# An in-projection that reads x in ready-made columns, takes four latent tiles in flight, and leaves the rope tables to the next stage

## The chip, the core and the metric

The kernel runs on one core of a Trainium2 chip. The time of a kernel is the device time of one launch in microseconds (us); times that are compared are medians over several executions. A core has a matmul engine (PE in the profile, with its weight loads as PEld), a vector engine (DVE, `V` in the code), an activation engine (ACT, `A`), a third elementwise engine (POOL, `G`) and a queue that issues most transfers (SP, `nc.sync`). Each engine works its own instructions off in the order in which the program wrote them, and waits for others by semaphores.

## The reference

One layer of a streaming encoder on x of 1024 rows by 1024 columns, all in float32:

```
h    = rmsnorm(x, g_mix);  proj = h @ w_in              # 1024 x 1952
c_q, c_kv, k_rope, qkv = proj[:, :256], [256:384], [384:416], [416:1952]
q    = rmsnorm(c_q) @ w_uq;  kv = rmsnorm(c_kv) @ w_ukv # 8 heads; per-head rmsnorm, rope
A    = block-causal attention(q, kv);  B = 9-chunk band attention(qkv) with a learned bias
x   += concat(rmsnorm(A), rmsnorm(B)) @ w_out
x   += w_down(silu(g) * u),  [g|u] = causal conv3(rmsnorm(x) @ w_up)
```

## The kernel before

Every float32 product is made of three faster ones (`mm3`, L136): each operand is split into a high part (rounded to the fast format) and a low part (what is left), and PE adds high by high, high by low and low by high. A split is one ACT or DVE instruction that writes the high part and one that subtracts it from the source.

The order on every engine is the order in which the Python code issues instructions (`manual_schedule`). Tiles come from pools: 28 buffers of 128x1024 (`blk`), 10 of 128x512 (`p2`), and banks of the matmul engine's accumulator. The stages that matter here:

**In-projection to the latents (loop at L408).** x comes in 8 tiles of 128 rows. PE needs x with its columns on the partitions, so `trans_x` (L213) transposes the eight 128x128 pieces of a tile on PE into a bank; ACT writes the high part and DVE the low part (`hTh`, `hTl`). `split_wlat` (L160) scales the four weight pieces of 416 columns by `g_mix` on ACT in place and splits them on DVE. `latent(t)` (L231) makes 24 matmuls of 416 columns, then ACT evicts the result, scales it by the row's 1/rms (`rsx`, from `norm_x`) and squares it in three pieces with an accumulator each; POOL turns each sum into 1/rms by a multiply-add and a power (`rsq`, L189), and DVE scales the latent. `trans_c(t)` (L252) transposes the latent on PE in three pieces, and ACT and DVE split it. In iteration t the order is `latent(t)`, `trans_x(t+2)`, `norm_x(t+2)`, `trans_c(t-1)`, and in iterations 2 to 5 one part of the rope tables: cosines and sines of the positions, with a transpose of small tables (L313 to L315), ten small DVE operations on the angles and a sine on ACT. `rope_k` (eight POOL operations) stands behind the loop.

**Up-projection of the latents (`up_mla`, L440, eight tiles)**, then **the other 1536 columns of the in-projection (L804)** in 32 steps, one for each 128 rows of 512 weight columns. In step i `load_wc(i+2)` loads weights that `split_wc(i+1)` (L533) splits: ACT scales in place, DVE casts the high part, DVE subtracts, in steps 26 to 31 POOL (`WC_LO_G`, L53). Steps from 3 on carry pieces of `side`, first of all `post_mla` (L489), which applies the rope tables on POOL.

**Entry to the attention (from step 22).** Between the matmuls of the last steps `prep` (L639) sets up the first two heads: transposes, splits into a tile `set`, and two copies on chip, `dup_q` (L678) and `dup_k` (L684), issued by POOL. The first products of the score maxima (`mx`, L724) read what `dup_k` writes.

The rest (attention, out-projection, a feed-forward part that is most of the time) is not touched.

Of the kernel before, what the change touches and what calls it, by code (L numbers as in the profile page):

```python
# [10 lines left out]
F32 = mybir.dt.float32  # L11
# [41 lines left out]
WC_LO_G = range(26, 32)  # L53
# [25 lines left out]
def trunk(ctx, tc, a, out):  # L79
# [62 lines left out]
    xt = {}  # L142
# [62 lines left out]
    gmix, rsx = scol(8), scol(8)  # L205
# [24 lines left out]

    def latent(t):  # L231
        p = bank()
        o = p[:, :LW]
        for k in range(8):
            h, c = hTv(0, t // 4), hTv(1, t // 4)
            s0 = (t % 4) * 128
            mm3(o, h[:, k, s0:s0 + 128], c[:, k, s0:s0 + 128], wlh[k // 2][:, k % 2, :LW], wll[k // 2][:, k % 2, :LW],
                k == 0, k == 7)
        l = blk(F32, "lat")
        lat[t] = l  # L240
        A.activation(l[:, :LW], o, AF.Copy, scale=rsx[:, t:t + 1])
        c = scol(4)
        A.activation(l[:, 512:768], l[:, 0:256], AF.Square, accum_out=c[:, 0:1])
        A.activation(l[:, 512:640], l[:, 256:384], AF.Square, accum_out=c[:, 1:2])
        A.activation(l[:, 512:544], l[:, 384:416], AF.Square, accum_out=ss_kr[:, t:t + 1])
        rsq(c[:, 2:3], c[:, 0:1], 1.0 / 256)
        rsq(c[:, 3:4], c[:, 1:2], 1.0 / 128)
        V.scalar_tensor_tensor(l[:, 0:256], l[:, 0:256], c[:, 2:3], lora_g[:, 0:256], op0=ALU.mult, op1=ALU.mult)
        V.scalar_tensor_tensor(l[:, 256:384], l[:, 256:384], c[:, 3:4], lora_g[:, 256:384], op0=ALU.mult, op1=ALU.mult)
        V.tensor_copy(KR[:, t, :], l[:, 384:416])  # L250

    def trans_c(t):  # L252
        p = bank()
        l = lat[t]
        for k in range(3):
            T.transpose(p[:, k * 128:(k + 1) * 128], l[:, k * 128:(k + 1) * 128], ident)
        if t < 6:
# [24 lines left out]
    def load_rows():  # L282
        rows = rope["rows"] = blk(F32, "rows")
        G.memset(rows[:, 0:256], 0.0)
        nc.sync.dma_start(rows[0:8, 256:384].bitcast(I32), a["positions"].rearrange("a (t p) -> (a t) p", p=128))
        nc.sync.dma_start(rows[:, 512:544], dap(a["g_mla_q"], NOPE, [[0, 128], [1, 32]]))
        nc.sync.dma_start(rows[:, 544:576], dap(a["g_mla_k"], NOPE, [[0, 128], [1, 32]]))
        nc.sync.dma_start(rows[0:128, 0:128], dap(a["conv_w"], 0, [[128, 128], [1, 128]]))
        nc.sync.dma_start(rows[0:4, 128:256], dap(a["conv_w"], 128 * 128, [[128, 4], [1, 128]]))
        nc.sync.dma_start(rows[4:48, 128:256], dap(a["conv_b"], 0, [[128, 44], [1, 128]]))  # L290
        nc.sync.dma_start(rows[48:52, 128:256], dap(a["g_out_mla"], 0, [[128, 4], [1, 128]]))
        nc.sync.dma_start(rows[52:56, 128:256], dap(a["g_out_ca"], 0, [[128, 4], [1, 128]]))
        nc.sync.dma_start(rows[56:57, 128:224], a["g_mla_q"])
        nc.sync.dma_start(rows[57:58, 128:224], a["g_mla_k"])
        nc.sync.dma_start(rows[58:59, 128:192], a["g_ca_q"])
        nc.sync.dma_start(rows[59:60, 128:192], a["g_ca_k"])
# [13 lines left out]
    def rope_angles():  # L310
        rows = rope["rows"]
        p = ps()
        T.transpose(p[:, 0:128], rows[:, 0:128], ident)  # L313
        T.transpose(p[:, 128:192], rows[0:64, 128:256], ident[0:64, 0:64])
        T.transpose(p[:, 192:200], rows[0:8, 384:512], ident[0:8, 0:8])  # L315
        V.tensor_copy(cols, p[:, 0:192])
# [5 lines left out]
        V.tensor_copy(pos, p[:, 192:200])  # L322
# [58 lines left out]
    def split_wq(i):  # L381
# [9 lines left out]
        V.tensor_tensor(l, s, f(h), op=ALU.subtract)  # L391
# [5 lines left out]
    T.transpose(p[:, 0:8], grow, ident[0:8, 0:8])  # L397
# [1290 lines left out]
```

## Time and profile before

| | |
|---|---|
| median of 3 runs | 1278.47 us (1276.62 to 1279.32) |
| profiled execution, own time | 1279.72 us |
| its span on the core | 1278.0 us, so 1.7 us lie around it |
| PE busy in the span | 1226.7 us (96%) |
| DVE, ACT, POOL busy | 942.8, 653.0, 699.1 us |
| granted clock of PE, mean over the span | 0.993 of full speed |

Times in the profile count from the start of the span. PE's matmuls overlap, so an instruction's own duration is longer than the distance to the next; what a matmul costs in a stream is that distance. [...]

### The profile page before, as it was taken

To read this page: it belongs to the slowest core of one execution; us is meant where nothing else is said; L and a number is where in the kernel's file an instruction comes from. 1 tells how busy PE (TensorE), PEld (TensorE's weight loads), DVE (VectorE), ACT (ScalarE), POOL (GpSimd) and SP (SyncE) were. 2 spreads that over 40 slices of the span, in tenths; PEclk is the share of its full clock that TensorE was granted. 3 is DMA by queue.
4 is the path that set the end of the run, shared out by engine and by line. 5 is a ranking of instruction groups with operands and counts; after the bars stand their busy time and mean duration, and the time that the engine had idled before them with its cause. 6 is when DMAs were issued, how large, how long until landed. Compare 5 with 4: busy or idle time off the path is not lost.

```text
span 1278.0 us, 17884 instructions
## 1 busy us (share of the span) xinstructions
PE 1226.7 (96%) x5920; PEld 1010.0 (79%) x5920; DVE 942.8 (74%) x1630; ACT 653.0 (51%) x1377; POOL 699.1 (55%) x715
## 2 busy tenths in 40 slices
PE   7999998899998998999989999999999999999998
PEld 7888886778786876788768888888888888878887
DVE  4786865778888895465898776677677677788983
ACT  6681443687877787504554444344344344434442
POOL 3578733455565668303568776676676650425630
PEclk9999998999999999999999999999999999999999
DMA  5101123111111121273513423323323246933253
GB/s 199 56 27 50 58 63 78 26 43 22 35 43 43 39 68 51 80 251 132 182 49 116 129 69 99 123 91 116 115 68 106 92 154 246 381 92 111 63 194 128
DMA packets 101316, 130.58 MB, mean 102 GB/s; under 512 B 11783, under 2 KB 60519, under 8 KB 101223
## 3 DMA queue, kind: packets, MB, share of 16 engines
q1 hardware_dynamic: 99431, 125.17, 30.3%
q0 software_dynamic: 1792, 4.26, 1.7%
q8 instruction: 47, 0.77, 0.3%
q14 instruction: 46, 0.38, 0.1%
HBM read 93.27 MB, written 31.81 MB: 98 GB/s over the span
## 4 chain that ended last, share of the span: by engine, by line
PE 50%; DVE 6%; POOL 2%; issue 2%; ACT 1%; POOLq 0%; DVEq 0%; ACTq 0%
PE pb L137 11%; PE pb L138 11%; PE pb L139 11%; PE ps L137 6%; PE ps L139 5%; PE ps L138 5%; DVE as L1404 1%; DVE ps L1420 1%; DVE x2b L1420 0%; DVE h L1188 0%; DVE as L1403 0%; DVE as L1405 0%; DVE as L1406 0%; POOL plo L932 0%; DVE wring L1595 0%
## 5 line engine op out<-in xcount | busy, mean ns | idle before, releaser
L932 POOL TENSOR_TENSOR plo<-misc,phi 128x512 fp32r<-128x512 f32 (+3 forms) x116 | 119.3, 1031 | 58.1 <-ACT phi L917 41.5
L1365 ACT ACTIVATE u<-ps,cols 128x1024 f32<-128x1024 f32 x44 | 53.2, 1208 | 177.7 <-DVE ps L1420 177.7
L137 PE MATMUL ps<-hq,wop 128*128 128x512 f32 x344 | 135.0, 392 | 2.6 <-ACT wop L1336 1.5
L139 PE MATMUL ps<-hq,wop 128*128 128x512 f32 x344 | 134.1, 390 | 1.2 <-DVE wop L1341 1.2
L138 PE MATMUL ps<-hq,wop 128*128 128x512 f32 x344 | 134.0, 390 | 0.1
L138 PE MATMUL pb<-wring,aring 128*128 128x512 f32 x308 | 120.1, 390 | 3.0 <-DVE wring L1595 3.0
L137 PE MATMUL pb<-wring,aring 128*128 128x512 f32 x308 | 120.0, 390 | 0.3 <-DVE x2b L1420 0.3
L139 PE MATMUL pb<-wring,aring 128*128 128x512 f32 x308 | 119.8, 389 | 0.0
L1341 POOL TENSOR_TENSOR wop<-S,wop 128x512 fp32r<-128x512 f32 x42 | 63.4, 1509 | 96.4 <-ACT wop L1336 96.4
L137 PE MATMUL pb<-hq,wop 128*128 128x512 f32 x264 | 103.5, 392 | 2.3 <-ACT wop L1336 2.3
L139 PE MATMUL pb<-hq,wop 128*128 128x512 f32 x264 | 103.7, 393 | 0.2 <-DVE wop L1341 0.2
L138 PE MATMUL pb<-hq,wop 128*128 128x512 f32 x264 | 103.2, 391 | 0.0
L1592 DVE TENSOR_TENSOR aring<-ast,aring 128x512 fp32r<-128x512 f32 x77 | 70.0, 909 | 36.8 <-ACT aring L1591 36.7
L1591 ACT ACTIVATE aring<-ast 128x512 fp32r<-128x512 f32 x77 | 48.5, 630 | 94.7 <-PE pb L138 75.4
L914 ACT ACTIVATE misc<-pb 128x512 f32<-128x512 f32 (+3 forms) x116 | 56.3, 485 | 48.4 <-PE pb L900 20.0
L137 PEld LDWEIGHTS ps<-hq,wop 128*128 128x128 f32 x344 | 64.6, 188 | 19.8 <-DVE ps L1420 4.9
L139 PEld LDWEIGHTS ps<-hq,wop 128*128 128x128 f32 x344 | 64.6, 188 | 15.2 <-DVE wop L1341 1.5
L137 PE MATMUL pb<-wh,hTh 128*128 128x512 f32 x192 | 76.3, 397 | 0.0
L138 PE MATMUL pb<-wl,hTh 128*128 128x512 f32 x192 | 76.0, 396 | 0.1
L139 PE MATMUL pb<-wh,hTl 128*128 128x512 f32 x192 | 75.5, 393 | 0.0
L138 PEld LDWEIGHTS ps<-hq,wop 128*128 128x128 f32 x344 | 64.6, 188 | 13.8 <-DVE hq L1224 0.6
L192 POOL TENSOR_TENSOR stat<-stat,mhalf 128x1 f32<-128x1 f32 (+2 forms) x50 | 71.6, 1431 | 4.2
(349 smaller groups left out, 3649.6 us busy)
## 6 DMA issues: line engine op xcount, KB each, us to landing
wstage<-in_w_up_dram SPq DMA_DIRECT2D x43, 512.0 KB
ast<-act_scratch SPq DMA_DIRECT2D x77, 256.0 KB
act_scratch<-as SPq DMA_DIRECT2D x44, 256.0 KB
wd<-in_w_down_dram SPq DMA_DIRECT2D x44, 256.0 KB
act_scratch<-u SPq DMA_DIRECT2D x33, 256.0 KB
x<-in_x_dram SPq DMA_DIRECT2D x16, 512.0 KB
ws<-in_w_in_dram SPq DMA_DIRECT2D x32, 256.0 KB
x_scratch<-x SPq DMA_DIRECT2D x14, 512.0 KB
```

Source lines behind the costliest of these rows:

```text
L137: T.matmul(o, lh, rh, start=start, stop=False)
L138: T.matmul(o, lh, rl, start=False, stop=False)
L139: T.matmul(o, ll, rh, start=False, stop=stop)
L192: G.tensor_tensor(dst, dst, mhalf[:, :n], op=ALU.pow)
L914: A.activation(p32[:, w], o[:, w], AF.Exp, scale=sc_)
L932: e.tensor_tensor(plo[:, w], p32[:, w], f(phi[:, w]), op=ALU.subtract)
L1341: (V if n in W_LO_V or (j, n) in W0_LO_V else G).tensor_tensor(lo, s, f(hi), op=ALU.subtract)
L1365: A.activation(u, U, AF.Identity, scale=convw(2, c), bias=convb(c))
L1404: V.tensor_tensor(s[1], s[0], A11, op=ALU.subtract)
L1420: V.tensor_tensor(d, x_, y, op=op)
L1591: A.activation(ah, s, AF.Copy)
L1592: V.tensor_tensor(al, s, f(ah), op=ALU.subtract)
```

## The change

The host now lays x out a second time, in columns (`x_cols`), and `g_mix`, the positions and the small tables as columns too. Each x tile is loaded twice: `xT` (columns) for `split_x`, which takes the place of `trans_x` and needs no PE, and `x` (rows) for `norm_x`. The loads stand in the order in which they are needed. Eighteen matmuls of the identity by itself run ahead of the first latent (`WARM`). The latent's work is cut into `latent`, `norm_lat`, `scale_lat`, `trans_c` and `split_c`, which in iteration t work on tiles t, t-1, t-1, t-2 and t-3. One square of 416 columns and three sums on DVE replace three squares with accumulators. The rope tables move to steps 0 to 3 of the next stage, and `split_wlat` and `split_wc` take two instructions in place of three (ACT writes the scaled high part, DVE makes scaled source minus high part); `WC_LO_G` is gone. The low part of `split_wq` moves from DVE to POOL.

```diff
-WC_LO_G = range(26, 32)
+WARM = 18
...
+    def load_xT(t, n=1):
+        xT[t] = blk(F32, "xT")
+        w = 1024 // n
+        for i in range(n):
+            nc.sync.dma_start(xT[t][:, i * w:i * w + w], a["x_cols"][t][:, i * w:i * w + w])
...
-        for k in range(2):
-            A.activation(s[:, k], s[:, k], AF.Copy, scale=gmix[:, 2 * i + k:2 * i + k + 1])
-        V.tensor_copy(wlh[i][:, :, :LW], s)
-        V.tensor_tensor(wll[i][:, :, :LW], s, f(wlh[i][:, :, :LW]), op=ALU.subtract)
+        for k in ks:
+            g = gmix[:, 2 * i + k:2 * i + k + 1]
+            hi = wlh[i][:, k, :LW]
+            A.activation(hi, s[:, k], AF.Copy, scale=g)
+            V.scalar_tensor_tensor(wll[i][:, k, :LW], s[:, k], g, f(hi), op0=ALU.mult, op1=ALU.subtract)
+
+    gmix = const([128, 8], F32, "gmix")
+    nc.sync.dma_start(gmix, a["g_mix_cols"])
     load_wlat(0)
-    load_wlat(1)
+    load_xT(0)
+    for i in range(1, 4):
+        load_wlat(i)
+    load_xT(1)
+    load_x(0)
+    load_xT(2)
     load_x(1)
...
-    def trans_x(src, t):
-        p = ps()
-        p3 = p.rearrange("p (k s) -> p k s", k=8)
-        for k in range(8):
-            T.transpose(p[:, k * 128:(k + 1) * 128], src[:, k * 128:(k + 1) * 128], ident)
+    def split_x(t, k0=0, k1=8):
+        p3 = xT[t].rearrange("p (k s) -> p k s", k=8)[:, k0:k1]
...
+    def norm_lat(t):
+        l = lat[t] = blk(F32, "lat")
+        c = clat[t] = scol(4)
+        A.activation(l[:, :LW], plat.pop(t)[:, :LW], AF.Copy, scale=rsx[:, t:t + 1])
+        sq = l[:, 512:512 + LW]
+        A.activation(sq, l[:, :LW], AF.Square)
+        for d_, c0, c1 in ((c[:, 0:1], 0, 256), (c[:, 1:2], 256, 384), (ss_kr[:, t:t + 1], 384, 416)):
+            V.reduce_sum(d_, sq[:, c0:c1], axis=AX)
         rsq(c[:, 2:3], c[:, 0:1], 1.0 / 256)
         rsq(c[:, 3:4], c[:, 1:2], 1.0 / 128)
...
         V.tensor_copy(h, s)
-        V.tensor_tensor(l, s, f(h), op=ALU.subtract)
+        G.tensor_tensor(l, s, f(h), op=ALU.subtract)
...
+    for _ in range(WARM):
+        T.matmul(p[:, 0:128], ident, ident, start=True, stop=True)
+    split_wlat(0)
+    split_x(0)
+    for i in range(1, 4):
         split_wlat(i)
+    split_x(1)
     norm_x(0)
...
+        latent(t)
+        if t >= 2:
+            trans_c(t - 2)
+        if t >= 1:
+            norm_lat(t - 1)
+        if t >= 3:
+            split_c(t - 3)
+        if t + 2 < 8:
+            split_x(t + 2)
+        if t + 1 < 8:
+            norm_x(t + 1)
         if t >= 4 and t < 7:
             split_wq(t - 4)
...
+            scale_lat(t - 1)
+    trans_c(6)
+    norm_lat(7)
+    split_c(5)
+    split_c(6)
+    scale_lat(7)
...
-            k = steps[i][1]
-            A.activation(s, s, AF.Copy, scale=gmix[:, k:k + 1])
+            g = gmix[:, steps[i][1]:steps[i][1] + 1]
             wh, wlo = p2(F32R, "wh"), p2(F32R, "wl")
-            V.tensor_copy(wh, s)
-            (G if i in WC_LO_G else V).tensor_tensor(wlo, s, f(wh), op=ALU.subtract)
+            A.activation(wh, s, AF.Copy, scale=g)
+            V.scalar_tensor_tensor(wlo, s, g, f(wh), op0=ALU.mult, op1=ALU.subtract)
...
+        if i < 4:
+            rope_tables(i)
+        if i == 3:
+            rope_k()
         if i:
             split_wc(i + 1)
```

What this does to the order on the engines shows at three places.

PE, between the third and the fourth latent before (`x` is the tile of rows that is transposed, `pb` an accumulator bank):

```order
L137 MATMUL pb_288<-wlh_130,hTh_89 128x416
L138 MATMUL pb_288<-wll_131,hTh_89 128x416
L139 MATMUL pb_288<-wlh_130,hTl_90 128x416
L217 MATMUL ps_325<-identr,x_211 128x128 x8
L256 MATMUL pb_340<-identr,lat_252 128x128 x3
L137 MATMUL pb_374<-wlh_112,hTh_89 128x416
```

PE at the same place after:

```order
L137 MATMUL pb_243<-wlh_142,hTh_94 128x416
L138 MATMUL pb_243<-wll_143,hTh_94 128x416
L139 MATMUL pb_243<-wlh_142,hTl_95 128x416
L273 MATMUL pb_268<-identr,lat_220 128x128 x3
L137 MATMUL pb_301<-wlh_122,hTh_94 128x416
```

The eight transposes of x are gone from PE, and the latent that is transposed is one tile older than before.

POOL at the entry to the attention before (`set` is the first head's tile, its two DMAs are `dup_q` and `dup_k`, `wl` the low part of a step's weights):

```order
L594 MEMSET set_2093 32x1024
L681 MEMSET set_2093 32x1024
L678 DMA set_2093<-set_2093 64x1024
L540 TENSOR_TENSOR wl_2119<-ws_2082,wh_2118 128x512
L684 DMA set_2093<-set_2093 64x1024
L540 TENSOR_TENSOR wl_2145<-ws_2115,wh_2144 128x512
```

POOL there after:

```order
L607 MEMSET set_2021 32x1024
L694 MEMSET set_2021 32x1024
L691 DMA set_2021<-set_2021 64x1024
L697 DMA set_2021<-set_2021 64x1024
L760 DMA set_2021<-mrow 1x8x128
```

The second copy no longer stands behind a subtraction of weights; the six subtractions are on DVE.

DVE in steps 2 and 3 of the next stage after (`rope` holds the angles, `wl_1180` is read by PE in step 3, `wl_1223` in step 4):

```order
L342 SCALAR_TENSOR_TENSOR rope_1069<-rope_1069 128x256 x5
L343 TENSOR_SCALAR rope_1069<-rope_1069 128x128
L344 TENSOR_SCALAR rope_1069<-rope_1069 128x256
L553 SCALAR_TENSOR_TENSOR wl_1180<-ws_1123,gmix,wh_1179 128x512
L354 TENSOR_TENSOR ropetabs_100<-rope_1069,rows_417 128x128
L355 TENSOR_TENSOR ropetabs_100<-rope_1069,rows_417 128x128
L356 TENSOR_TENSOR ropetabs_100<-rope_1069,rows_417 128x128
L357 TENSOR_TENSOR ropetabs_100<-rope_1069,rows_417 128x128
L553 SCALAR_TENSOR_TENSOR wl_1223<-ws_1164,gmix,wh_1222 128x512
```

The reduction of the angles now stands ahead of the weights of step 3, and the tables ahead of those of step 4; before, these were in the in-projection loop.

## Rows read from the trace of the kernel before

**Rows 1.** Busy time by stretch; columns: length, PE, PEld, DVE, ACT, POOL, clock, DMA share, GB/s.

```profile
22.60:58.00 35.40, 34.88 (x209) 33.48 (x208) 23.53 (x57) 24.68 (x65) 18.02 (x52) 1.00 0.28 101
58.00:88.00 30.00, 28.79 (x150) 26.27 (x149) 24.64 (x86) 24.50 (x108) 21.86 (x29) 1.00 0.04 10
88.00:206.60 118.60, 118.52 (x527) 96.74 (x525) 82.28 (x143) 45.85 (x102) 78.06 (x87) 1.00 0.22 61
...
210.80:216.30 5.50, 5.50 (x15) 4.41 (x16) 2.40 (x9) 0.00 (x0) 1.28 (x1) 0.50 0.15 38
```

**Rows 2.** Timeline of PE in the in-projection: start, duration, instruction, [idle before].

```profile
8.96 1.94 PE L217 MATMUL ps<-identr,x 128*128 128x128 f32 x8 [2.09 <-DMA x<-in_x_dram]
...
14.17 0.55 PE L138 MATMUL pb<-wll,hTh 128*128 128x416 f32 x1
...
14.52 0.55 PE L139 MATMUL pb<-wlh,hTl 128*128 128x416 f32 x1
...
22.43 0.36 PE L139 MATMUL pb<-wlh,hTl 128*128 128x416 f32 x1
...
23.74 0.43 PE L137 MATMUL pb<-wlh,hTh 128*128 128x416 f32 x1
...
28.35 1.03 PE L217 MATMUL ps<-identr,x 128*128 128x128 f32 x8
...
29.22 0.49 PE L256 MATMUL pb<-identr,lat 128*128 128x128 f32 x3
...
35.27 0.27 PE L313 MATMUL ps<-identr,rows 128*128 128x128 f32 x1
...
35.83 0.46 PE L137 MATMUL pb<-wlh,hTh 128*128 128x416 f32 x1
```

**Rows 3.** Waits of PE up to 300 us: total, times, longest.

```profile
PE pb L724 <- DMA set<-set: 4.2, 1, 4.2
...
PE pb L137 <- DVE cTl L264: 1.2, 1, 1.2
```

**Rows 4.** Same columns as the first group, for the first loads (last column GB/s).

```profile
0.00:3.00 3.00, 0.00 (x0) 0.00 (x0) 0.23 (x1) 1.28 (x1) 0.74 (x7) 1.00 0.30 63
3.00:9.00 6.00, 2.18 (x10) 1.82 (x11) 1.20 (x2) 2.09 (x4) 0.00 (x0) 1.00 1.02 377
```

**Rows 5.** Groups of instructions in the first 62 us: busy us, mean ns.

```profile
L192 POOL TENSOR_TENSOR stat<-stat,mhalf 128x1 f32<-128x1 f32 x24 | 15.9, 664 | 2.0
...
L221 ACT ACTIVATE hTh<-ps 128x1024 fp32r<-128x1024 f32 x8 | 8.1, 1009 | 4.8 <-PE ps L217 4.8
...
L222 DVE TENSOR_TENSOR hTl<-ps,hTh 128x1024 fp32r<-128x1024 f32 x8 | 9.8, 1219 | 2.8 <-ACT hTh L221 2.8
...
L248 DVE SCALAR_TENSOR_TENSOR lat<-lat,stat,lorag 128x256 f32<-128x256 f32 x8 | 3.9, 483 | 13.1 <-POOL stat L192 13.1
...
L249 DVE SCALAR_TENSOR_TENSOR lat<-lat,stat,lorag 128x128 f32<-128x128 f32 x8 | 2.8, 352 | 4.8 <-POOL stat L192 4.8
```

**Rows 6.** Timeline of ACT and of POOL at the entry to the attention.

```profile
202.66 0.59 ACT L669 ACTIVATE set<-pb 64x512 fp32r<-64x512 f32 x1
...
203.81 1.28 POOL L540 TENSOR_TENSOR wl<-ws,wh 128x512 fp32r<-128x512 f32 x1 [1.04 <-DVE wh L539]
...
205.05 0.58 POOL L684 DMA_DIRECT2D set<-set  x1
```

**Rows 7.** All eight `dup_k` copies of the kernel (line L684).

```profile
DMA to landing us min/median/max: 2.9/3.0/5.6
```

**Rows 8.** Timeline of DVE: first and last of the angles' reduction, eleven instructions.

```profile
45.94 0.22 DVE L331 TENSOR_SCALAR rope<-rope 128x128 f32<-128x128 f32 x1
...
49.82 0.29 DVE L341 TENSOR_SCALAR rope<-rope 128x256 f32<-128x256 f32 x1
```

**Rows 9.** Timeline of POOL: the seventh rope job of `side`.

```profile
135.14 3.45 POOL L501 TENSOR_TENSOR rt<-nqk,ropetabs 128x128 f32<-128x128 f32 x4 [5.09 <-DVE nqk L493]
```

**Rows 10.** Timeline of POOL: one power in the in-projection's sixth iteration.

```profile
53.80 1.93 POOL L192 TENSOR_TENSOR stat<-stat,mhalf 128x1 f32<-128x1 f32 x1
```

More of the change, by code (lines that the diff above doesn't have):

```diff
@@ L229, in trunk @@
     ss_kr = scol(8)
+    plat, clat = {}, {}
     def latent(t):
-        p = bank()
-        o = p[:, :LW]
+        p = plat[t] = bank()
         for k in range(8):
@@ L236, in latent, with scale_lat @@
             s0 = (t % 4) * 128
[L237 to L245, printed above, removed]
+            mm3(p[:, :LW], h[:, k, s0:s0 + 128], c[:, k, s0:s0 + 128], wlh[k // 2][:, k % 2, :LW],
+                wll[k // 2][:, k % 2, :LW], k == 0, k == 7)
+    def norm_lat(t):
[6 more added lines that the diff above has]
+            V.reduce_sum(d_, sq[:, c0:c1], axis=AX)
         rsq(c[:, 2:3], c[:, 0:1], 1.0 / 256)
         rsq(c[:, 3:4], c[:, 1:2], 1.0 / 128)
+    def scale_lat(t):
+        l, c = lat[t], clat[t]
         V.scalar_tensor_tensor(l[:, 0:256], l[:, 0:256], c[:, 2:3], lora_g[:, 0:256], op0=ALU.mult, op1=ALU.mult)
@@ L250, in latent @@
         V.tensor_copy(KR[:, t, :], l[:, 384:416])
+    pcT = {}
     def trans_c(t):
-        p = bank()
+        p = pcT[t] = bank()
         l = lat[t]
@@ L256, in trans_c, with split_c @@
             T.transpose(p[:, k * 128:(k + 1) * 128], l[:, k * 128:(k + 1) * 128], ident)
+    def split_c(t):
+        p = pcT.pop(t)
         if t < 6:
@@ L283, in load_rows @@
         rows = rope["rows"] = blk(F32, "rows")
[L284 to L285 removed]
+        nc.sync.dma_start(cols[:, 0:188], a["cols"])
+        nc.sync.dma_start(rows[:, 0:8].bitcast(I32), a["pos_cols"])
         nc.sync.dma_start(rows[:, 512:544], dap(a["g_mla_q"], NOPE, [[0, 128], [1, 32]]))
         nc.sync.dma_start(rows[:, 544:576], dap(a["g_mla_k"], NOPE, [[0, 128], [1, 32]]))
[L288 to L296, printed above, removed]
     def rope_tables(part):
@@ L310, in rope_angles @@
     def rope_angles():
[L311 to L316, printed above, removed]
         V.tensor_tensor(gsc[0:64, 0:1], cols[0:64, GQ:GQ + 1], cols[0:64, GK:GK + 1], op=ALU.mult)
@@ L321, in rope_angles @@
         pos = rt[:, 512:520]
-        V.tensor_copy(pos, p[:, 192:200])
+        V.tensor_copy(pos, rope["rows"][:, 0:8].bitcast(I32))
         inv = rt[:, 528:544]
@@ L396, in trunk @@
     p = ps()
-    T.transpose(p[:, 0:8], grow, ident[0:8, 0:8])
-    V.tensor_copy(gmix, p[:, 0:8])
-    trans_x(xt[0], 0)
-    for i in range(4):
+    for _ in range(WARM):
[3 more added lines that the diff above has]
+    for i in range(1, 4):
         split_wlat(i)
+    split_x(1)
     norm_x(0)
@@ L404, in trunk @@
     nc.sync.dma_start(lora_g[:, 256:384], dap(a["g_kv_lora"], 0, [[0, 128], [1, 128]]))
-    trans_x(xt[1], 1)
-    norm_x(1)
     for t in range(8):
         if t + 3 < 8:
-            load_x(t + 3)
-        if t == 1:
-            load_rows()
+            load_xT(t + 3)
+        if t + 2 < 8:
+            load_x(t + 2)
         if t == 3:
             load_wq()
+        if t == 5:
+            load_rows()
+        latent(t)
[5 more added lines that the diff above has]
+            split_c(t - 3)
+        if t + 2 < 8:
+            split_x(t + 2)
+        if t + 1 < 8:
+            norm_x(t + 1)
         if t >= 4 and t < 7:
             split_wq(t - 4)
-        latent(t)
-        if t + 2 < 8:
-            trans_x(xt[t + 2], t + 2)
-            norm_x(t + 2)
         if t >= 1:
-            trans_c(t - 1)
-        if 2 <= t < 6:
-            rope_tables(t - 2)
-    rope_k()
+            scale_lat(t - 1)
[4 more added lines that the diff above has]
+    scale_lat(7)
     side = []
@@ L775, in trunk @@
             trans_c(7)
+            split_c(7)
         if t == 2:
@@ L1678 @@
     arrays, args = {}, {}
+    inputs = {n: np.asarray(v) for n, v in inputs.items()}
+    pad = [np.pad(inputs[n].reshape(1, -1), ((0, 0), (0, 128 - inputs[n].size)))
+           for n in ("g_mla_q", "g_mla_k", "g_ca_q", "g_ca_k")]
+    inputs["cols"] = np.concatenate([inputs[n].reshape(-1, 128) for n in ("conv_w", "conv_b", "g_out_mla", "g_out_ca")]
+                                    + pad).T
+    inputs["pos_cols"] = inputs["positions"].reshape(NT, 128).T
+    inputs["x_cols"] = inputs["x"][0].reshape(NT, 128, 8, 128).transpose(0, 3, 2, 1).reshape(NT, 128, D)
+    inputs["g_mix_cols"] = inputs["g_mix"].reshape(8, 128).T
     for n, v in inputs.items():
```

34 lines of the change are left out of this document (15 added, 19 removed).

## The prediction

> **What bounds the kernel now.** First I read the table of engines by stretch [rows 1]. PE is busy for 34.88 of the 35.40 us of the later in-projection, for 28.79 of 30.00 in the up-projection and for 118.52 of 118.60 in the 32 steps that follow; no other engine comes near. From 22.6 us to the entry of the attention the time is therefore PE's own: an instruction taken from PE is time gained, and work taken from DVE, ACT or POOL is worth only what PE waited for it. Three places are different.
>
> The first 22.6 us, read from the timeline of PE [rows 2]: PE waits 2.09 us for the second tile of x, then works latent(0) with matmuls .35 us apart (14.17 to 14.52), and latent(1)'s last one starts at 22.43. In a stream later on 24 matmuls take 28.35 - 23.74 = 4.61 us, .19 apart. So the start is set by loads, by splits and by a slow clock together.
>
> The second is up_mla(0), where PE waits 1.2 us for the last split of a latent [rows 3].
>
> [...]
>
> **The change, part by part.** All sums are against the profiled execution's own 1279.72 us; the runs' median is 1.25 lower.
>
> *Start.* By the traffic [rows 4], 3.0 x 63 GB/s = .19 MB came up to 3.0 us and then .377 MB each us. Before, x(0) with g_mix (.528 MB) is through at 3.9 and x(1), at 1.904 MB, at 7.55; PE sees x(1) at 8.96, so 1.4 us later [rows 2]. After, xT(0) ends at .954 MB (5.0), the last weights at 2.23 MB (8.4), xT(1) at 2.756 MB (9.8). With .8 to 1.4 us until it is seen, xT(0) is there at 5.9 to 6.4 and xT(1) at 10.6 to 11.2. ACT's high part takes 1.01 and DVE's low part 1.22 [rows 5]: latent(0) can start at 7.2 and has its low part at 8.4. Behind that DVE has six of the eight new weight instructions of 416 columns. Their form's rows are .483 for 256 columns and .352 for 128 [rows 5], so .131 for 128 more, and .65 for 416 is my estimate: 6 x .65 = 3.9, to 12.3. The low part of xT(1) is done at 13.5. Only each third matmul of latent(1) needs that, so it starts some .4 earlier and ends near 13.1 + 4.5 = 17.6, where before it ended at 22.6. **-5.0.** [...]
>
> The 18 WARM matmuls run ahead of that, on a tile that waits for no load. No row has a plain float32 matmul of 128 columns. A transpose of 128 is .11 (.87 for eight, from 28.35 to 29.22 [rows 2]), which gives 2 us below; .25 for each, as if it took two to three passes, gives 4.5. Begun within the first 2 us, they end between 4 and 6.5, before latent(0) can start. Even at .5 each they would end near 11, and latent(1) would lose under 1.5, since DVE holds it to 13.1.
>
> *Transposes.* Eight for a tile cost .87 [rows 2]. Those of tiles 0 and 1 lie in the start. Of the other six, that of x(2) stood ahead of 22.6 and is counted there; five in the stretch 22.6 to 58 are removed: 5 x .87 = 4.35. The rope transposes take 35.83 - 35.27 = .56. **-4.9**, between 0 and -4.9 as far as other engines keep up. They have the room: DVE is busy 23.53 and ACT 24.68 of 35.40 [rows 1]; of that the rope tables leave. What the new order adds is one latent of distance to norm_lat, trans_c and split_c, 4.5 us for each, so that a chain of POOL's powers has longer. PE's idle .52 in this stretch goes too: **-.5**.
>
> *Up-projection.* The wait of 1.2 was for the last latents. After, seven of the eight latents are transposed before up_mla(0), and norm_lat(7) and scale_lat(7) stand ahead: **-.9** (-.5 to -1.2). But trans_c(6) now stands directly behind latent(7), and waits until POOL has made the powers of latent 6, which had one latent's time; a chain of evict, square, three sums, two times two POOL instructions of .66 [rows 5] and two scales is some 5.5 us against 4.5 of cover: **+.5** (0 to +1.5).
>
> *Rope tables in steps 0 to 3.* They take 4.2 us of DVE (45.94 to 50.11 [rows 8]) ahead of wl(3) in step 2, and four products ahead of wl(4). A step is 118.60/32 = 3.7 us of PE on the average, and DVE works 82.28 of 118.60 there [rows 1] and loses 32 x some .3 by splitting with one instruction instead of two. The splits run a step ahead of PE. I work out that wl(3) is finished some 3 us ahead of its use: **0** (0 to +3). The rope jobs on POOL come later, by up to 5.4 us; the seventh waited 5.09 for DVE anyway [rows 9]: 0. The split itself (one instruction less) frees DVE and ACT, which PE does not wait for: 0; the cover is PE's 118.52 of 118.60.
>
> *Entry.* Before, ACT writes the high part at 202.66 to 203.25; POOL then has wl from 203.81 to 205.09, and issues `dup_k` at 205.05 [rows 6]. A copy takes 2.9 to 5.6 us from issue to landing [rows 7]; this one was the long one, since PE went on at 210.8. After, `dup_k` stands right behind `dup_q` and is issued near 203.3: 1.75 earlier. With a landing of 3 us it would be there at 206.3, before PE is through with the steps (206.6); I take the wait to go from 4.2 to 1.0, since something of the longer landing was the traffic around it, and it need not go: **-3.2** (0 to -4.2). A shorter wait should spare part of the dip; half of the 2.7 is my choice: **-1.5** (0 to -2.7). That PE stays at full clock through a gap is shown once, in the wait of 1.2 us in up_mla(0): the stretch 58 to 88 has 1.00 throughout [rows 1, 3].
>
> Sum: -5.0 - 4.9 - .5 - .9 + .5 - 3.2 - 1.5 = -15.5, so 1264.2 on the profile's scale and **1263.0** on that of the median.
>
> **The rivals.**
>
> *The entry stays as it is.* dup_k's landing is governed by the traffic then and not by its issue, or another part of `set` is late. For it: 5.6 is far from the median of 3.0 [rows 7], and the stream of loads runs on. Against it: an issue 1.75 earlier is plain in POOL's order. Price 3.2 + 1.5 = 4.7: 1267.7.
>
> *POOL holds the in-projection.* It gets three subtractions of `split_wq`, at 1.28 for 512 columns [rows 6], in iterations 4 to 6. A power took 1.93 there once [rows 10], against .66 in the mean [rows 5]: while DVE worked on two operands from the core's memory. After, all x splits of DVE read such operands, where before one came from an accumulator bank. Each latent has three powers; all stretched to 1.93 make its chain 3.8 longer, with a subtraction ahead of it 5.1. Of the two latents of time that trans_c has, 9.2 us, the chain of some 5.5 leaves 3.7: only the three iterations with subtractions would wait, 1.4 us each and as much again in what they pass on to up_mla(0): +5, 1268. Against it: not all powers meet such a split. [...]
>
> *Rope holds the steps.* wl(3) comes behind 4.2 us of angles, and if my margin of 3 us is wrong PE waits in step 3: +3, 1266.
>
> [...]
>
> **How the numbers follow.** The forecast has 55%, with its own range of 1261 to 1266. The entry unchanged has 20% (1267.7), POOL 13% (1268), rope 7% (1266), the clock 4% (1294), and 1% is left for a change that is eaten without trace. The lower end, 1259.5, takes the whole wait (-1.0 more), the whole dip (-1.2) and the better start and up-projection (-.5 and -.8); the upper, 1269.0, holds the entry or POOL with a little more. About 0.2% (2.6 us) is what a measurement of this kernel can tell from no change. Faster by over that: .95; within it .01; slower .04.
>
> **What the profile would show.** Start: latent(1)'s last matmul at about 17.6, spacing .19 from the first or after a few matmuls. Transposes: up_mla(0) starts near 58 - 10.4 + .5 = 48, and no idle row in the loop. Entry: the wait on `mx` for `dup_k` at 1 us or gone, and the row with clock .50 shorter, near 195. Rope: no wait of PE on wl in steps 2 to 5. Wrong is the forecast if PE waits for lat or cT in the loop (POOL), if `mx` still waits 4 us, or if a stretch ahead of 40 us has a clock of .50.

## The result, and the profile after

The changed kernel takes 1270.16 us (median of 4 runs, 1268.70 to 1271.62) against 1278.89 for the kernel before beside it: a ratio of .9934 [.9921, .9947], 8.7 us less. In a second set of five runs it took 1270.95. The forecast was 1263.0, which is 15.9 us below that median (its sum was 15.5). So the gain is real and about half of what the sum gave, and the time lies above the stated range.

The profiled execution has a span of 1269.9 us, 8.1 below the one before. Its timeline of PE shows where (start, duration, instruction, idle before and what ended it):

```profile
8.46 0.43 PE L137 MATMUL pb<-wlh,hTh 128*128 128x416 f32 x1
...
14.27 0.45 PE L139 MATMUL pb<-wlh,hTl 128*128 128x416 f32 x1 [0.62 <-DVE hTl L231]
...
18.32 0.35 PE L139 MATMUL pb<-wlh,hTl 128*128 128x416 f32 x1
...
49.19 0.41 PE L273 MATMUL pb<-identr,lat 128*128 128x128 f32 x2 [1.40 <-ACT cT L283]
...
50.16 0.33 PE L273 MATMUL pb<-identr,lat 128*128 128x128 f32 x1 [0.57 <-DVE lat L264]
...
50.25 0.42 PE L137 MATMUL pb<-wq,cT 128*128 128x384 f32 x1
...
184.63 0.50 PE L138 MATMUL pb<-wl,hTh 128*128 128x512 f32 x1 [1.21 <-DVE wl L553]
...
189.31 0.50 PE L138 MATMUL pb<-wl,hTh 128*128 128x512 f32 x1 [0.74 <-DVE wl L553]
...
202.97 0.76 PE L737 MATMUL pb<-set 128*128 128x256 f32 x2 [3.61 <-DMA set<-set]
```

The first matmul of latent(0) starts at 8.46, the last one of latent(1) at 18.32; at 50.25 begins up_mla(0). Against [rows 1, 2] and the wait of [rows 3] this gives the ledger of the profile, stage by stage:

| stage, on PE | before | after | moved | forecast |
|---|---|---|---|---|
| start, to the last matmul of latent(1) | 22.43 | 18.32 | -4.1 | -5.0 |
| from there to up_mla(0) | 35.57 | 31.93 | -3.6 | -4.9 (-4.9 - .5 + .5) |
| up_mla, to the first step | 30.00 | 28.59 | -1.4 | -.9 |
| steps, to the end ahead of `mx` | 118.6 | 120.52 | +1.9 | 0 |
| wait of `mx` for `dup_k` | 4.2 | 3.61 | -.6 | -3.2 |
| clock behind it and the rest | 1067.2 | 1066.93 | -.3 | -1.5 |

The row of the steps ends ahead of the first product of `mx`; the last 22 of the steps' 192 groups of three matmuls stand behind it, in the last row.

The same by stretches (length, PE, PEld, DVE, ACT, POOL, clock, DMA share, GB/s):

```profile
18.70:47.30 28.60, 28.60 (x160) 28.16 (x160) 20.40 (x49) 19.58 (x34) 25.24 (x38) 1.00 0.59 226
50.25:78.84 28.59, 28.59 (x148) 26.29 (x149) 24.89 (x88) 23.07 (x102) 18.40 (x21) 1.00 0.07 20
78.84:199.36 120.52, 118.55 (x527) 96.92 (x525) 82.72 (x139) 47.23 (x102) 88.70 (x110) 1.00 0.21 57
199.36:202.97 3.61, 0.01 (x1) 0.04 (x1) 0.00 (x0) 0.00 (x0) 0.00 (x0) 0.86 0.94 198
202.97:208.40 5.43, 5.43 (x14) 4.38 (x15) 2.73 (x9) 0.72 (x1) 0.00 (x0) 0.50 0.15 42
```

These rows answer to [rows 1]. POOL is busy for 25.24 of 28.60 us in the in-projection, where it had been 18.02 of 35.40. In the steps PE is idle for 2 us of 120.52, where it had missed .1. The stretch behind the entry has the clock at .50 for 5.4 us, as before.

### The profile page after: what moved, and what is told of

The parts are those of the page before. It is cut to its first block, busy times and chain, and to the rows that moved or that the text cites. A ratio compares the mean times of both kernels' runs of the same rounds, so it can differ in the third digit from the quotient of the medians.

```text
span 1269.9 us, 17774 instructions
## 1 busy us (share of the span) xinstructions
PE 1221.0 (96%) x5888; PEld 1004.7 (79%) x5888; DVE 940.8 (74%) x1623; ACT 648.8 (51%) x1338; POOL 704.6 (55%) x710
## 4 chain that ended last, share of the span: by engine, by line
PE 50%; DVE 8%; issue 2%; ACT 1%; POOL 1%; DVEq 0%; POOLq 0%; ACTq 0%
PE pb L139 11%; PE pb L138 11%; PE pb L137 11%; PE ps L137 6%; PE ps L139 5%; PE ps L138 5%; DVE ps L1438 1%; DVE as L1422 1%; DVE hq L1242 1%; POOL plo L950 1%; DVE wop L1359 1%; DVE h L1206 0%; DVE as L1421 0%; DVE as L1423 0%; DVE as L1424 0%
```

## The experiments

All are the changed kernel with one edit, unless said otherwise. Single executions differ by several us in parts that no edit touches: what stands behind the first product of `mx` took 1064.8 to 1068.1 us in seven profiled executions whose edit, if any, lies ahead of it, and the way from the last matmul of latent(7) to up_mla(0) took 2.97 to 4.87 us in eight that have the changed kernel's code there. Medians of a few runs, taken in different sets, therefore blur what is worth 2 us; each verdict rests on the place in the trace first and on the time second.

**Three places were open:** 2 us ahead of up_mla(0), 1.9 us in the steps, and the entry.

**1. One subtraction given back to DVE.** POOL's rows around the wait at 49.19 in the changed kernel:

```profile
45.23 2.38 POOL L394 TENSOR_TENSOR wkl<-wks,wkh 128x1024 fp32r<-128x1024 f32 x1
47.70 0.19 POOL L203 TENSOR_SCALAR stat<-stat 128x1 f32<-128x1 f32 x1
47.97 0.55 POOL L204 TENSOR_TENSOR stat<-stat,mhalf 128x1 f32<-128x1 f32 x1
...
49.17 0.55 POOL L204 TENSOR_TENSOR stat<-stat,mhalf 128x1 f32<-128x1 f32 x1
```

The subtraction of `split_wq`'s third piece lies in front of the two powers of latent 6, at 47.97 and 49.17. The edit:

```diff
-        G.tensor_tensor(l, s, f(h), op=ALU.subtract)
+        (V if i == 2 else G).tensor_tensor(l, s, f(h), op=ALU.subtract)
```

> The changed kernel, with the low part of the third piece of split_wq (1024 columns, iteration 6) on DVE again instead of POOL; all else as changed. Theory: in the changed kernel POOL is busy with that subtraction for 2.38 us (45.23 to 47.61) just when the powers of latent 6 are due, DVE waits 2.8 us for them, and PE waits 1.40 and .57 us in trans_c(6). Then both waits of PE shrink to under .4 together, up_mla(0) starts near 48.4 instead of 50.25, and the time is 1.9 us below the changed kernel's, near 1268.3. Rival: the chain of latent 6 (evict, square, sums, two powers, two scales) is too long for one latent of cover whatever POOL does first: the waits keep at least 1.2 us and the time stays within .8 us of the changed kernel's 1270.2.

Measured: 1269.17 (.9935 [.9913, .9958]); PE still waits 1.35 and .57. up_mla(0) starts at 49.52, but only because latent(7) ended .7 us earlier in this execution: from latent(7)'s last matmul it is 3.10 us, as against 3.15. The theory in this form fell: the subtraction held DVE for 1.23 us ahead of its scales, one power of POOL beside it took 1.53 us, and POOL was at work up to the powers of latent 6 all the same. What was left was a backlog.

**2. One power less for each latent**, and **3. all of `split_wq` on DVE again**:

```diff
-        rsq(c[:, 2:3], c[:, 0:1], 1.0 / 256)
-        rsq(c[:, 3:4], c[:, 1:2], 1.0 / 128)
+        G.tensor_scalar(c[:, 2:3], c[:, 0:1], 1.0 / 256, EPS, op0=ALU.mult, op1=ALU.add)
+        G.tensor_scalar(c[:, 3:4], c[:, 1:2], 1.0 / 128, EPS, op0=ALU.mult, op1=ALU.add)
+        G.tensor_tensor(c[:, 2:4], c[:, 2:4], mhalf[:, 0:2], op=ALU.pow)
```

```diff
-        G.tensor_tensor(l, s, f(h), op=ALU.subtract)
+        V.tensor_tensor(l, s, f(h), op=ALU.subtract)
```

> The changed kernel, with the two powers of a latent made by one instruction of two columns on POOL instead of two of one column; all else as changed. The run with one subtraction given back to DVE kept PE's waits ahead of trans_c(6), so the theory now is a backlog: POOL works without a gap from about 30 to 50 us, and the powers of latent 6 stand at its end, whatever piece is taken out near it. A power less for each latent (about .63 us with the gap behind it, seven times) shortens the backlog by some 4 us: PE's waits ahead of trans_c(6) (1.97 us in the changed kernel, 3.4 in two of the runs since) fall below .8, from the last matmul of latent(7) to up_mla(0) it takes 1.5 us or less instead of 3.15, and the time is 1.5 to 2.5 below 1270.2. Rival: the latency of one latent's own chain sets it; the waits stay at 1.5 or more and the time within .8 of 1270.2.

> The changed kernel, with the low parts of all three pieces of split_wq on DVE again, as before the change. Theory of the backlog on POOL: 6 us of POOL's work between 35 and 48 us go, POOL has idle time in iterations 5 to 7, and from the last matmul of latent(7) to up_mla(0) it takes 1.6 us or less, where it took 3.15 in the changed kernel and 1.16 with the powers merged. Rival: the subtractions of two operands on DVE (about 1 us each) hold POOL as much as they free it, as in the run with one of them: 2.7 or more.

All waits of PE between latent(6) and the steps, first with merged powers, then with `split_wq` on DVE:

```profile
47.33 0.52 PE L274 MATMUL pb<-identr,lat 128*128 128x128 f32 x3 [0.22 <-DVE lat L264]
...
49.33 0.50 PE L137 MATMUL pb<-wkh,cT 128*128 128x512 f32 x1 [0.42 <-DVE cT L285]
```

```profile
49.31 0.50 PE L137 MATMUL pb<-wkh,cT 128*128 128x512 f32 x1 [0.83 <-DVE cT L284]
```

From the last matmul of latent(7) to up_mla(0) it takes 1.16 and .77 us, where it took 3.15 (2.97 to 4.87 in the eight executions with the changed kernel's code there). A wait of .4 or .8 comes up in up_mla(0) instead, for the split of a latent; to the first step it is 30.39 and 30.38 us, against 31.55 to 35.69 in the eight. So both rivals fall, and that of run 1 with them. The times are 1269.46 (.9942 [.9928, .9957]), which is less of a gain than forecast and within the .8 us that the rival had named, and 1267.74 (.9928 [.9914, .9941]). With merged powers the first product of `mx` comes 2.0 us sooner (200.96), but what stands behind it took 1.2 us longer.

The place is settled by the trace. Here is the last power of latent 6 on POOL in runs 1, 2 and 3:

```profile
48.45 0.55 POOL L204 TENSOR_TENSOR stat<-stat,mhalf 128x1 f32<-128x1 f32 x1
```

```profile
45.96 0.70 POOL L260 TENSOR_TENSOR stat<-stat,mhalf 128x2 f32<-128x2 f32 x1
```

```profile
45.56 0.55 POOL L204 TENSOR_TENSOR stat<-stat,mhalf 128x1 f32<-128x1 f32 x1
```

Counted from the start of latent(7)'s last matmul (46.42, 46.44 and 46.41) it ends 2.58 us behind it, .22 behind it, and .30 ahead of it; in the eight it is 2.44 to 4.30 behind. From latent(1)'s last matmul to the end of that power POOL is busy for 26.5 to 28.0 us in the eight, and for 27.8, 20.7 and 23.6 in the three runs. So one subtraction of 2.4 us given away took nothing off POOL that shows, since its other instructions became longer beside DVE's (the one power 1.53 in place of .55); of all three, 6.1 us, some 3 to 4.5 came off, since a power beside two of DVE's took up to 2.13. POOL had more work than the shorter stage leaves it.

**4. The normalisation one job later, and 5. three instructions for a split again.** In the steps, the rows of DVE and of POOL ahead of PE's wait at 184.63:

```profile
178.01 1.23 DVE L541 TENSOR_TENSOR ca<-ca,stat 128x1024 f32<-128x1024 f32 x1 [1.66 <-POOL stat L204]
...
179.16 0.74 DVE L553 SCALAR_TENSOR_TENSOR wl<-ws,gmix,wh 128x512 fp32r<-128x512 f32 x1
...
182.69 1.23 DVE L541 TENSOR_TENSOR ca<-ca,stat 128x1024 f32<-128x1024 f32 x1 [2.79 <-POOL stat L204]
...
183.83 0.75 DVE L553 SCALAR_TENSOR_TENSOR wl<-ws,gmix,wh 128x512 fp32r<-128x512 f32 x1
```

```profile
178.06 1.24 POOL L203 TENSOR_SCALAR stat<-stat 128x16 f32<-128x16 f32 x1
179.39 3.27 POOL L204 TENSOR_TENSOR stat<-stat,mhalf 128x16 f32<-128x16 f32 x1
182.74 1.24 POOL L203 TENSOR_SCALAR stat<-stat 128x16 f32<-128x16 f32 x1
```

DVE waits for the power, then normalises from 178.01 to 179.24; POOL's next multiply-add starts at 178.06 and ends at 179.30, 1.24 us for 16 columns; then the power; and so on, 4.68 us a round against a step of 2.7. The low part of the weights (L553) stands behind the normalisation and comes late. The two edits:

```diff
-        if j > 1:
-            n3 = ca[c, j - 2]...
+        if j > 2:
+            n3 = ca[c, j - 3]...
...
-                for j in range(6):
+                for j in range(7):
...
-SIDE_2 = 5, 6, 8
+SIDE_2 = 5, 6, 8, 9
```

```diff
-            wh, wlo = p2(F32R, "wh"), p2(F32R, "wl")
-            A.activation(wh, s, AF.Copy, scale=g)
-            V.scalar_tensor_tensor(wlo, s, g, f(wh), op0=ALU.mult, op1=ALU.subtract)
+            A.activation(s, s, AF.Copy, scale=g)
+            wh, wlo = p2(F32R, "wh"), p2(F32R, "wl")
+            V.tensor_copy(wh, s)
+            V.tensor_tensor(wlo, s, f(wh), op=ALU.subtract)
```

> The changed kernel, with the normalisation in post_ca one job later (tile j-3 in place of j-2, seven jobs instead of six, one more step with two jobs). Theory: in steps 18 to 23 DVE waits for POOL's power of the tile that it is about to normalise (2.79 us each), and its normalisation of 1.23 us then starts together with POOL's next multiply-add, which takes 1.24 instead of .2; so the chain takes 4.68 us a step against 2.74 of PE, and the low part of the weights, queued behind the normalisation, comes late. With one job more of distance DVE does not wait there: its waits ahead of the normalisation fall from 14.0 us to under 5, PE's waits for wl (1.21 and .74) go, and the time is near 1268.3. Rival: DVE and POOL have too much work in these steps in any order: PE still waits 1.5 us or more for wl, and the time is within .8 us of 1270.2.

> The changed kernel, with split_wc in its three instructions again (ACT scales in place, DVE casts, DVE subtracts), all on DVE. Theory of the lockstep: the shorter split let DVE arrive at the normalisation before POOL's power; with the longer one DVE comes later, waits less than 6 us there instead of 14.0, most of POOL's multiply-adds in these steps are under .6 us again, and PE's waits for wl in steps 18 to 23 are under .5 together: near 1268.5. Rival (plain overload of DVE): more work on DVE makes the same waits longer, 2.5 us or more: 1271 or above.

In the kernel before, POOL's four multiply-adds of this place took .31, .20, .21 and 1.24 us: it had the long one only at the end. With three instructions they are short again until the last:

```profile
175.90 0.21 POOL L203 TENSOR_SCALAR stat<-stat 128x16 f32<-128x16 f32 x1
...
179.17 0.21 POOL L203 TENSOR_SCALAR stat<-stat 128x16 f32<-128x16 f32 x1
...
182.44 1.24 POOL L203 TENSOR_SCALAR stat<-stat 128x16 f32<-128x16 f32 x1
```

DVE's waits for the power fall from 14.0 to 4.3 us, and PE waits for no wl in steps 16 to 23. With more work on DVE the wait goes: plain overload is excluded. In return PE waits .21 and .51 for wh and wl in step 3 (at 96.37 and 97.37), where the rope tables stand on DVE; the time is 1270.51 (.9944 [.9923, .9964]), so the edit saves one wait and pays another.

With one job more of distance PE's waits for wl are gone as well (1268.41, .9928 [.9905, .9951]), but DVE still waits 10.1 us for powers, against 14.0, where I had said under 5:

```profile
184.98 1.23 DVE L541 TENSOR_TENSOR ca<-ca,stat 128x1024 f32<-128x1024 f32 x1 [2.79 <-POOL stat L204]
...
189.66 1.23 DVE L541 TENSOR_TENSOR ca<-ca,stat 128x1024 f32<-128x1024 f32 x1 [2.20 <-POOL stat L204]
```

The lockstep is there still; its last round only ends early enough. That the waits come from it is shown; that more distance dissolves it is not. The stretch itself repeats well: from the first step to the wait for `dup_k` it is 118.56 us in the kernel before, 120.50 to 120.55 in ten executions that leave this code as changed, 119.73 with three instructions and 117.70 with the job more (117.65 in the repaired kernel of run 11).

**6 to 8. What is beside `dup_k`.** At the entry, POOL's two copies, SP's issues, and the landing over the eight `dup_k`:

```profile
195.28 0.78 POOL L691 DMA_DIRECT2D set<-set  x1 [0.99 <-ACT set L674]
196.85 0.54 POOL L697 DMA_DIRECT2D set<-set  x1 [0.80 <-ACT tb L715]
```

```profile
196.88 0.33 SPq L712 DMA_DIRECT2D tb<-bias_scratch  x1
197.29 1.25 SPq L526 DMA_DIRECT2D ws<-in_w_in_dram  x2
```

```profile
DMA to landing us min/median/max: 2.9/3.1/6.0
```

The largest of the eight, 6.0, is the first head's. `dup_k` is issued at 196.85, .31 us after the high part of k is ready (ACT, 195.95 + .59), where it had been 1.80 [rows 6]; it lands 6.0 us later. SP issues the bias table (128 KB) and two weight loads (256 KB each) at the same moment. Three runs take traffic away: the loads of steps 28 and 29 left out (`e3_noload`, which uses the weights of step 27 again), the bias load earlier (`e3_early`), and both (`e3_quiet`, with the same work left out).

```diff
     def load_wc(i):
+        if i in (28, 29):
+            wch[i] = wch[i - 1]
+            return
```

```diff
-              ... (6, "post", bias_nat), (6, "post", lambda: bias_load(1)), ...
+              ... (6 if n else 0, "post", bias_nat), (6 if n else 0, "post", lambda: bias_load(1)), ...
```

> The changed kernel, which leaves out the loads of the weights of steps 28 and 29 (256 KB each) and uses those of step 27 again there, so that only the table of biases (128 KB) travels beside dup_q and dup_k. Theory: dup_k's landing of 6.0 us is the traffic of these two loads, which SP issues at 197.29, .4 us after dup_k. Then dup_k lands in 2.9 to 3.6 us, the wait of mx falls from 3.61 to about 1, the stretch at .50 gets shorter or goes, and the time is 2.5 to 5 us below the changed kernel's: 1265 to 1267.7. Rival one: dup_k stands behind dup_q in POOL's queue of copies, whatever SP does: the landing stays above 5 and the wait above 3, the time at 1270. Rival two: the load of the bias table, of rows of 1 KB that overlap, is the one in the way: the landing is between 4 and 5, the wait about 2, and the time near 1268.5.

> The changed kernel, in which the first head's bias_nat and the second load of its bias table stand at slot 0 in place of slot 6, so that this load of 128 KB goes out some 10 us ahead of dup_q and dup_k, and the weight loads that stood behind it on SP are free to go when their buffers are. Theory: dup_k lands late because it shares the DMA engines with that load and the ones that it held back. Then dup_k's landing falls from 6.0 to 4 or less, PE's wait for it from 3.61 to 1.5 or less, and the time by 2 to 4 us from 1270.2. If the buffers of the weight loads come free only at the same moment, they still collide: landing about 5, wait about 2.6, as without two of these loads. Rival: it is POOL's own queue: landing 6, wait 3.5.

> Both: the bias load early as in the run beside it, and the weight loads of steps 28 and 29 left out (the weights of step 27 are used again), so that dup_q and dup_k travel almost alone. Theory of traffic: landing 2.9 to 3.3 us, as the least of the eight, the wait of mx .8 us or less, and no stretch at .50 behind it; the time 4 to 6 us below 1270.2. Rival: dup_k waits behind dup_q in POOL's queue of copies: landing 4.5 or more and a wait of 2 or more even without other traffic.

| run | landing | wait of `mx` | time, ratio |
|---|---|---|---|
| changed kernel | 6.0 | 3.61 | 1270.16, .9934 |
| e3_early | 6.1 | 3.98 | 1274.40, .9978 [.9969, .9987] |
| e3_noload | 5.2 | 2.78 | 1270.68, .9945 [.9925, .9965] |
| e3_quiet | 3.8 | 1.76 | 1265.86, .9919 [.9902, .9936] |

In `e3_quiet` the first head's copy lands in 3.8 us; the 4.1 that the text of run 9 has for it is the second head's:

```profile
DMA to landing us min/median/max: 3.8/3.8/3.8
```

`e3_early` missed: the bias load went out only 3 us ahead of `dup_k` (195.00 and 198.00), and the weight loads, three of them now, from 195.42 to 198.99, right beside both copies; `dup_q` landed in 6.2 us there, where it had been 3.1. `e3_noload` came out between its theory and its first rival; its time is no lower because the way from latent(7) to the first step, which the edit does not touch, took 34.65 us in its execution, 2.9 more than in the changed kernel's. In `e3_quiet` the wait and the slow stretch go together:

```profile
200.28 0.65 PE L740 MATMUL pb<-set 128*128 128x256 f32 x3 [1.76 <-DMA set<-set]
```

```profile
200.28:205.70 5.42, 5.42 (x31) 4.65 (x31) 4.22 (x14) 1.30 (x2) 0.00 (x0) 1.00 0.00 0
```

Landing and wait fall with each load that is taken away, though not to the forecast of 2.9 to 3.3; even there SP issued one more weight load at 197.19, .9 us after `dup_k`.

**9. `dup_k` on SP, ahead of the loads**, nothing left out:

```diff
-            G.dma_start(st.K1[0:64], st.K2[0:64])
+            if n == 0:
+                nc.sync.dma_start(f(st.K1[0:64]), f(st.K2[0:64]))
+            else:
+                G.dma_start(st.K1[0:64], st.K2[0:64])
```

> The changed kernel, with the first head's dup_k issued by SP (the same bytes, read as plain float32) ahead of the bias load and the weight loads of steps 28 and 29, in place of POOL; nothing is left out. In the runs before, dup_k landed in 6.0, 5.2 and 4.1 us as fewer loads travelled beside it, and PE waited 3.6, 2.8 and 1.8. Theory: it is the share of the DMA engines that the loads behind it take. Ahead of them in the same queue dup_k lands in about 3 us from 196.6, PE waits .7 or less, and the stretch at .50 is shorter than 2 us or gone: 3 to 5 us below 1270.2. Rival: ahead in the queue is not ahead on the engines, which work off several transfers side by side: landing 4.5 or more, wait 2 or more, less than 2 us gained.

SP's issues, PE's wait, and the stretch behind it:

```profile
195.86 0.54 SPq L698 DMA_DIRECT2D set<-set  x1
196.50 0.55 SPq L715 DMA_DIRECT2D tb<-bias_scratch  x1
```

```profile
199.20 0.65 PE L740 MATMUL pb<-set 128*128 128x256 f32 x3 [0.53 <-DMA set<-set]
```

```profile
199.20:204.60 5.40, 5.40 (x30) 4.63 (x31) 3.99 (x14) 2.02 (x3) 0.00 (x0) 1.00 0.48 150
```

PE goes on 3.3 us after the issue, where it had been 6.1. The wait is .53 and the clock stays at 1.00; 1266.69 (.9916 [.9902, .9930]), against 1270.95 for the changed kernel in the same set. The run doesn't part the place in the queue from the kind of queue, since both were changed.

**10. No WARM matmuls** (`WARM = 0`).

> The changed kernel without the WARM matmuls. Theory: they give the first latent the high clock, as the spacing of .19 from 8.46 us on shows; without them latent(0) begins about 7.5 at .35 a matmul, the clock rises some 5 us later, and latent(1) ends near 19.5 instead of 18.5. Since POOL's backlog and not PE sets the end of this stage, up_mla(0) comes at most .6 later: 1270.2 to 1270.9. [...] Rival (cover): nothing in this stage waits for PE, and the time is the same or lower.

The first matmuls of latent(0):

```profile
7.61 0.72 PE L137 MATMUL pb<-wlh,hTh 128*128 128x416 f32 x1 [7.61 <-ACT hTh L230]
...
10.42 0.55 PE L137 MATMUL pb<-wlh,hTh 128*128 128x416 f32 x1
...
11.33 0.35 PE L137 MATMUL pb<-wlh,hTh 128*128 128x416 f32 x1
...
11.52 0.35 PE L138 MATMUL pb<-wll,hTh 128*128 128x416 f32 x1
```

They start at 7.61, .35 apart once the low part of x is there, and are .19 apart from 11.33 on. In the kernel before, too, they are .35 apart from 11.05 to 14.86, and the granted clock from 10.56 to 14.86 is 1.00; so the slow clock that the prediction names for the start shows in the distances alone. latent(1)'s last one starts at 18.49, against 18.32 and 17.70 in two executions with WARM, and up_mla(0) at 50.15 against 50.25 and 49.60: 1271.58 (.9961 [.9947, .9974]). WARM is worth under 1 us of PE's start, and at up_mla(0) nothing of it is left to see. The time lies .7 us above the theory's range, but its interval overlaps that of the changed kernel's second set (run 12), so theory and cover can't be told apart by it.

**11. The three repairs together** (merged powers, normalisation a job later, `dup_k` on SP), beside **12. the changed kernel again**.

> The changed kernel with three repairs together: the two powers of a latent in one instruction, the normalisation in post_ca one job later, and the first dup_k on SP ahead of the loads. If each works in its own stage, the trace shows 1.2 us from latent(7) to up_mla(0), no wait for wl in the steps and under .8 us for dup_k, and the time is the changed kernel's less 2.0, 1.95 and 3 to 5: 1261.3 to 1263.3. If the gains run into each other (what comes earlier waits at the entry again), 1265 or more.

> The changed kernel once more, as it is, beside the others on this chip: 1270.2 within 1.5 us, a gap of 3.1 to 4.7 us from the last matmul of latent(7) to up_mla(0) (3.15 in its first profile, 4.6 and 4.7 in two runs with the same code there), two waits for wl of 1.2 and .7, and 3.6 for dup_k.

Measured: 1261.64 (.9880 [.9865, .9895]) against 1270.95 (.9947 [.9935, .9960]); all waits of PE for these three things in the repaired kernel (total, times, longest):

```profile
PE pb L137 <- DVE cT L285: 0.8, 1, 0.8
...
PE pb L741 <- DMA set<-set: 0.6, 1, 0.6
```

It takes .76 us from the last matmul of latent(7) to up_mla(0), PE waits for no wl in the steps, and the first product of `mx` starts at 195.44, against 202.97 and 203.69 in the changed kernel's two profiles. The time lies in the range for gains that add up, and the version is faster than both kernels. By their medians, taken in different sets, the three edits alone had brought only .7, 1.75 and 3.5 us. The changed kernel's own second profile has the waits as expected (1.39 and .57 ahead of up_mla(0), 1.19 and .75 for wl, 3.52 for `dup_k`).

## Why the prediction was wrong, by its steps

**Entry: -3.2 - 1.5 forecast, -.6 and about 0 measured.** This is the step that failed most. It took the landing as 3 us, because that is the median of the eight copies, and put the long one down to traffic that would stay behind. The row in [rows 7] said 5.6, and the copy kept it: SP's loads wait for the same moment (bias_nat on ACT, just behind the high part of k; SP's first issue comes .34 us behind that in both kernels) and move with `dup_k`. Of the 1.5 us of earlier issue, .4 went to the longer landing and .5 to PE, which now comes that much sooner after the high part of k to its wait. It was the rival "the entry stays as it is", at 20%. In the changed kernel `dup_q`'s packets go out alone and `dup_k`'s beside SP's; here by queue (packets, MB, share; q0 is POOL's), for 196.50 to 198.10, 198.50 to 201.70 and 201.70 to 202.85 us:

```profile
q0 software_dynamic: 80, 0.26, 81.9%
...
q1 hardware_dynamic: 199, 0.28, 53.9%
q0 software_dynamic: 80, 0.26, 33.9%
...
q1 hardware_dynamic: 125, 0.22, 87.4%
```

So `dup_q` took 1.6 us for its 80 packets and `dup_k` 3.2 us for as many. `dup_k`'s first packet comes some 1.7 us after its issue, `dup_q`'s 1.2 after its own; that it stands behind `dup_q` in POOL's queue, the rival of three runs, can have cost about half a microsecond and no more. All of `dup_k`'s packets were through by 201.70, and it landed at 202.85; in between only SP's queue had packets, 125 of them at 87.4%. What kept the landing for these 1.15 us no run isolates.

The dip's -1.5 is about half of 2.7 us, and the 2.7 is an estimate, half of the 5.50 us at .50 in [rows 1]. No run shows this term. In its place the changed kernel, with .6 us less of wait, has 5.43 us at .50, as before. The size of 2.7 agrees with the runs: at .50 PE began 14 matmuls in 5.43 us, at 1.00 it began 31 in 5.42 (`e3_quiet`) and 30 in 5.40 (`e6_spq`). The dip went with the wait: with waits of .53, .56 and 1.76 the granted clock of the next 5.4 to 5.5 us was 1.00; with waits of 3.61 and 4.21 (the changed kernel and the one before) it was .50; with 2.78 (`e3_noload`) it was .64 for 1.82 us, .50 for the next 2.00 and .97 for 2.00 more.

**Steps: 0 forecast, +1.9 measured.** "The split itself (one instruction less) frees DVE and ACT, which PE does not wait for: 0" failed. It counted the work of DVE and not its order: a faster DVE reached the normalisation ahead of POOL's power and waited there with the weights queued behind it, and the two engines fell into step. No rival had this. The average step of 3.7 us hid the place, too: the first sixteen steps take PE 5.4 us each and the others 2.7, against 4.68 for a round of DVE and POOL. Of the rope tables the step was right: PE waits for no wl in steps 0 to 4 of the changed kernel.

**trans_c(6): +.5 forecast (0 to 1.5), 2.0 measured.** The mechanism was named, but the price came from the chain of one latent alone. It was the backlog of POOL, the rival at 13%, at less than its price of 5: 6.1 us of subtractions (1.86, 1.85 and 2.38, where the rival had 1.28 for each) in a stage that had become shorter. The wait can cost more than it shows: behind the same wait the clock stayed at 1.00 in the changed kernel's first profile, and in its second that of the next 5.4 us was .68, and the up-projection took 30.07 us instead of 28.59:

```profile
49.60:55.00 5.40, 5.40 (x23) 4.94 (x23) 4.36 (x18) 0.91 (x3) 2.82 (x11) 0.68 0.00 0
```

**Start: -5.0 forecast, -4.1 and -4.7 measured**, a term a little too large: in the first profile latent(1) waited .62 us, at 14.27, for its low part. The 18 matmuls of WARM took 6.7 us, from 1.73 to 8.46, above both bounds of 2 and 4.5, and held latent(0) to 8.46, where it starts at 7.61 without them; it cost little, as worked out. The range's .5 us for a still better start no run shows; the two starts gained .9 and .3 us less than the term. The clock, at 4%, did not hold the in-projection: the changed kernel's matmuls are .19 apart from 8.73 on, and its granted clock is 1.00 up to 40 us. **Transposes and idle: right.** From the last matmul of latent(1) to that of latent(7) it was 35.13 us and is 28.78, 6.3 less against 5.4 forecast (one transpose of a latent, .3, has also moved behind latent(7)). From 18.7 to 47.3 PE has no gap. **Up-projection: -.9 forecast (-.5 to -1.2), -1.4 measured.**

With the three mis-sized terms repaired, the kernel takes 1261.64, 15.4 us less than the kernel before beside it (1277.04). The gains that the sum listed were there, and the new order of POOL, DVE and SP took about half of them back. That 15.4 meets the sum of 15.5 is in part luck, since the terms do not meet one by one: the entry gives more than forecast (a wait of .56 and no dip), and the start less.

## What to carry to other kernels

An instruction that becomes shorter can change which engine arrives first (here DVE came to wait 14.0 us for powers): look at what its engine waits for next, and at what stands behind that wait, before the saved work is priced at nothing. A transfer that is issued earlier need not take less time if the loads beside it are released by the same event (`dup_k`, issued 1.5 us sooner after the high part of k, took 6.0 us in place of 5.6); put the urgent one ahead of them (3.3 us from issue to PE in place of 6.1, by SP), and take its landing from the copy at that place rather than from the median of all. When a stage gets shorter, add up each helper engine's busy time against the new length, POOL's above all (here 25.24 of 28.60 us, where it had been 18.02 of 35.40).

## What the runs showed of the hardware

A multiply-add of 16 columns on POOL took .20 and .21 us beside a DVE reduction of one operand (at 182.75 and 186.02 in the kernel before), and in the changed kernel 1.24 when it began with a DVE instruction on two operands from the core's memory; there it ended .06 us after that instruction, twice in a row (179.30 behind 179.24, 183.98 behind 183.92). My rival had a power stretched from .66 to 1.93 us; this instruction took six times as long, and ended with DVE's both times. Why, no run isolates.

A plain float32 matmul of 128 columns took .37 us (18 of them, in 36 records, from 1.73 to 8.46), and .31 to .38 in other executions, about as much as three transposes of .11.
